# Regrouping the token blocks of a hybrid decoder step from 3+3+3 to 3+4+2, with a second buffer pool for the last group

## The chip, the core and the metric

One core of a Trainium2 chip runs the whole program. The time is that of one execution on the device, in microseconds; a run's number is the median of its executions. The engines named below are TensorE (PE; its weight loads are listed apart as PEld), VectorE (DVE), ScalarE (ACT), GpSimd (POOL) and SyncE (SP), which here only issues DMAs. Each engine works through its own list of instructions in order and waits on semaphores; which instruction stands where in a list is fixed when the program is built.

## The reference

One layer is run for a prompt of 1024 tokens and for a sample group of 8 x 8 tokens, with the same weights, everything in float32. Cut to what matters:

```python
n = rmsnorm(x, g_mix)
z = n @ w_in                      # 1024 x 7192: GLA, FoX, memory queries, three gates
h = x + (sum over b of sigmoid(gate_b) * (branch_b(n) @ w_b)) @ w_out
q = rmsnorm(h, g_ffn) @ w_pq      # 8 heads, two halves of 128
s1, s2 = q_half @ k1.T, q_half @ k2.T
v1, i1 = top_k(s1, 16); v2, i2 = top_k(s2, 16)
sc, pos = top_k(v1[:, None] + v2[None, :], 16)     # 16 of 16384 experts per head
g = softmax(sc)
a = gelu(x . u_tab[idx])          # 128 experts per token
h = h + sum (g * a) * v_tab[idx]
y = rmsnorm(h, g_final)
```

Two ways lead through the expert part. A block of 128 tokens can fetch, for each of its 128 expert slots, one row of `u` and one of `v` per token by an indirect DMA and work on them with VectorE (it is gathered). Or it can run all 16384 experts as dense matmuls against a weight matrix that is zero except at the chosen experts (it goes through the tables).

## The kernel before

The tokens are nine blocks: prompt blocks 0 to 7 of 128 tokens, and block S with the 64 sample tokens. `GROUPS` runs them in three groups through `base` (line 633), which reads every weight matrix once per group: input projection, the three branches, the gates, `w_out`, the second norm, `w_pq` and the key products. Each weight piece of 128x512 is split into a rounded part `wh` (ScalarE, line 265) and a rest `wl` (VectorE, line 267); three matmuls then stand for one. Two kinds of projection use it: `proj` puts 256 weight columns through one block at a time, `proj_T` (`jobs_T`, lines 273 to 277) puts all tokens of the group, NT of them, through 128 weight columns, so the width of its matmuls is NT. With the key products the scores of each head go to VectorE, where `top16` (lines 932 to 936) takes the 16 best of 128 twice per head and block; the blocks in `LATER` store their scores and do this inside `choose` instead.

`choose` picks the 16 pairs per head and their softmax weights. For a gathered block `peer_gather` follows (lines 1052 to 1094): 128 times an indirect DMA on POOL's queue (line 1065) brings u rows, which VectorE multiplies and sums (line 1067), and 128 times v rows (line 1076), which VectorE accumulates (line 1082). Four row buffers are shared by the two, a fifth is added in the last phase, and one block's gather follows the other. For a block in `DENSE`, `expert_weights` (line 1096) builds the weight matrix: one-hot rows on VectorE and ScalarE, a matmul into the PSUM tile `cw`, an eviction to the tile `stg` (line 1143), and after 16 tokens a DMA of `stg` to DRAM (`c_scr`). The sample block's weights are built in the last phase.

The last phase, `peer_dense` (lines 1148 to 1256), runs the 128 expert tiles for the 448 tokens of `DENSE`: per tile 8 transposes of `u`, 24 matmuls with `u` and 24 with `v`, all 448 wide. It starts when `early.close()` has given back the pools of the first part. Beside it the remaining gathered blocks are gathered.

What sets the order is a scheduler at build time with one priority per instruction. `base` of all groups counts up from zero and goes first; `choose` and `expert_weights` of the earlier groups start at half a million (`urgent`) and fill in; the gathers lie at a million and more and take what is left. So before, blocks 0, 1 and 2 are gathered beside the second and third `base`, and 6 and 7 beside the dense phase. Tiles of the first part come from the pool `bp`, whose tags hold a fixed number of buffers (`BUFS`, `CB`); `wr` holds raw weight pieces and the sample's cache pages, `P` wide scratch.

Of the kernel before, what the change touches and what calls it, by code (L numbers as in the profile page):

```python
# [18 lines left out]
F32 = mybir.dt.float32  # L19
# [19 lines left out]

ROWS, ROWS2 = 4, 5  # L40
SAMPLE = 8
GROUPS = [[0, 1, 2], [3, 4, 5], [SAMPLE, 6, 7]]

DENSE = [3, 4, 5, SAMPLE]

LATER = [6, 7]

HERE = [SAMPLE]
DG, DW = 8, 9
WR = 4  # L50
CB = {"hot": 4, "stg": 1, "eg": 1}


@with_exitstack
def tile_hybrid(ctx: ExitStack, tc: tile.TileContext, x_prompt, x_sample, cache_fox_k, cache_fox_v,
# [10 lines left out]
    dp = ctx.enter_context(tc.tile_pool(name="dp", bufs=1, space=bass.MemoryType.DRAM))  # L66
    gp = ctx.enter_context(tc.tile_pool(name="gp", bufs=1))
    early = ctx.enter_context(ExitStack())
    ec = early.enter_context(tc.tile_pool(name="ec", bufs=1))
    pp = early.enter_context(tc.tile_pool(name="pp", bufs=8, space=bass.MemoryType.PSUM))  # L70
    bp = early.enter_context(tc.tile_pool(name="bp", bufs=1))

    BUFS = {"aT": 2, "wr": WR, "wh": 4, "wl": 2, "z": 4, "zq": 1, "zt": 4, "tq": 2, "tp": 3, "oT": 3, "kv": 2, "pg": 2,
            "la": 2, "ge": 3, "lh": 4, "kE": 2, "gq": 1, "att": 2, "X": 2, "XL": 2, "P": 4, "PT": 3, "sm": 12,
            "sm2": 1, "sm5": 1}
    PSB = {"pj": 2, "g": 2, "f": 2, "po": 1, "cw": 1}
    cnt = [0]

    def T(tag, shape, dt=F32):
        cnt[0] += 1  # L80
        return bp.tile(shape, dt, tag=tag, name=f"{tag}_{cnt[0]}", bufs=BUFS[tag])

    def const(shape, dt=F32, pool=ec):
        cnt[0] += 1
# [538 lines left out]
    s_scr = {b: dp.tile([128, 2048], F32, name=f"s_scr{b}") for b in LATER}  # L623
    e_scr = {b: dp.tile([128, 128], I32, name=f"e_scr{b}") for b in DENSE}
    g_scr = {b: dp.tile([128, 128], F32, name=f"g_scr{b}") for b in DENSE}
    c_scr = dp.tile([sum(64 if b == SAMPLE else 128 for b in DENSE) // 16, 128, 2048], F32, name="c_scr")
    q_scr = dp.tile([128, 4, 64], F32, name="q_scr")
    x2_scr = [dp.tile([128, 1024], F32, name=f"x2_scr{b}") for b in range(9)]

    gate_scr = [dp.tile([12, 128, 2, 384], F32, name=f"gate_scr{i}") for i in range(len(GROUPS))]  # L630
    o_scr = [dp.tile([128, 3, 4, 128], F32, name=f"o_scr{b}") for b in range(9)]

    def xsrc(b):
# [4 lines left out]
    def base(grp):  # L638
# [64 lines left out]

        gscr = gate_scr[GROUPS.index(grp)]
        gates = gate_jobs()
# [5 lines left out]
        for half in range(2):  # L711
# [56 lines left out]
            def fin_k(b, p):  # L768
# [11 lines left out]
                evac(kT[:, :, b * 128:(b + 1) * 128], pt[:, :256].rearrange("p (j t) -> p j t", t=128))  # L780
                if b < 7 and grp is not GROUPS[-1]:
                    SP.dma_start(kT_scr[half * 256:(half + 1) * 256, b * 128:(b + 1) * 128].rearrange(
# [161 lines left out]
    def choose(b):  # L944

        if b not in DENSE:
            eidx[b] = gp.tile([128, 128], I32, tag="ei", name=f"ei{b}", bufs=2)
            gate_w[b] = gp.tile([128, 8, 16], F32, tag="gw", name=f"gw{b}", bufs=2)
        for hf in range(2):
# [52 lines left out]
            c = slice(hf * 64, (hf + 1) * 64)  # L1002
            if b in DENSE:
                ei, gw = w[:, 528:592].bitcast(I32), region(656, 16)
# [91 lines left out]
    def expert_weights(b, H=None, psum=None):  # L1096

        w = 64 if b == SAMPLE else 128
        o = sum(64 if x == SAMPLE else 128 for x in DENSE[:DENSE.index(b)]) // 16

        def H_base(tag, shape, dt=F32):
            cnt[0] += 1
            return bp.tile(shape, dt, tag=tag, name=f"{tag}_{cnt[0]}", bufs=CB[tag])

        H = H or H_base
        psum = psum or (lambda: PS("cw"))


        q, e, f = H("hot", [128, 2, 128]), H("hot", [128, 2, 128]), H("hot", [128, 2, 128])
        qi = q[:, 0].bitcast(I32)  # L1110
        SP.dma_start(qi, e_scr[b])
        SP.dma_start(q[:, 1], g_scr[b])
        V.tensor_scalar(e[:, 0].bitcast(I32), qi, 7, None, op0=OP.logical_shift_right)
        V.tensor_scalar(e[:, 1].bitcast(I32), qi, 127, None, op0=OP.bitwise_and)
        V.tensor_copy(f, e.bitcast(I32))
        p = psum()
        for i, src in enumerate((f[:, 0], f[:, 1], q[:, 1])):
            PE.transpose(p[:, i * 128:(i + 1) * 128], src, ident)

        eg = H("eg", [128, 4, 128])  # L1120
        for i in range(4):
            j = min(i, 2)
            A.activation(eg[:, i, :w], p[:, j * 128:j * 128 + w], AF.Copy, scale=-1.0 if i == 3 else 1.0)
        for sb in range(w // 16):
            stg = H("stg" if H is H_base else "c", [128, 128, 16])
            for q2 in range(8):
                ts = [sb * 16 + q2 * 2 + i for i in range(2)]
                o2, o1 = H("hot", [128, 2, 128]), H("hot", [128, 2, 128])
                for i, t in enumerate(ts):
                    if q2 % 2:  # L1130
                        V.tensor_scalar(o2[:, i], iof, eg[:, 1, t:t + 1], eg[:, 2, t:t + 1], op0=OP.is_equal,
                                        op1=OP.mult)
                    else:

                        A.activation(o2[:, i], iof, AF.Square, scale=-1.0, bias=eg[:, 1, t:t + 1])
                        A.activation(o2[:, i], o2[:, i], AF.Relu, scale=eg[:, 3, t:t + 1], bias=eg[:, 2, t:t + 1])
                V.tensor_tensor(
                    o1, iof[:, None, :].to_broadcast([128, 2, 128]),
                    eg[:, 0, ts[0]:ts[0] + 2, None].to_broadcast([128, 2, 128]), op=OP.is_equal)
                p = psum()  # L1140
                for i, t in enumerate(ts):
                    PE.matmul(p[:, i * 128:(i + 1) * 128], o2[:, i], o1[:, i], start=True, stop=True)
                A.activation(stg[:, :, q2 * 2:q2 * 2 + 2].rearrange("p n t -> p t n"),
                             p[:, :256].rearrange("p (t n) -> p t n", t=2), AF.Copy)
            SP.dma_start(c_scr[o + sb], stg.rearrange("p n t -> p (n t)"))

    def peer_dense(ctx2, dn):
# [31 lines left out]
        for b in DENSE:  # L1179
            if b in GROUPS[-1]:  # L1180
                expert_weights(b, DT, lambda: DP("c"))
# [16 lines left out]
        for g in range(128 // DG):  # L1198
            if g * DG % 8 == 0:
                c8 = DT("c", [128, NS, 128])  # L1200
                ready = NS - sum(w for b, w in zip(DENSE, widths) if b in GROUPS[-1]) // 16
                for x in (slice(0, ready), slice(ready, NS)) if g == 0 else (slice(0, NS),):
# [261 lines left out]

    for grp in GROUPS:
        pj3[0] = grp is GROUPS[0]
        base(grp)
        mine = [b for b in grp if b not in DENSE]
        first = [b for b in grp if b in DENSE]
        if grp is not GROUPS[-1]:  # L1470
            first = mine[:1] + first
        else:
            first += mine[:1]
        for b in first:
            if b in DENSE and grp is GROUPS[-1]:
                choose(b)
            else:
                at(None, choose, b)
            if b in DENSE and grp is not GROUPS[-1]:
                at(None, expert_weights, b)  # L1480
        if mine and grp is not GROUPS[-1]:
            gather(mine)
# [38 lines left out]
```

## Time and profile before

| what | value |
|---|---|
| three runs | 4328.08, 4340.33, 4341.13 us (median 4340.33) |
| the profiled execution | 4325.89 us |
| its span, first to last instruction | 4324.1 us |
| mean granted TensorE clock | 0.909 of full |
| PE busy | 3719.4 us (86%) |
| DVE busy | 3338.8 us (77%) |
| ACT busy | 1821.1 us (42%) |
| POOL busy | 1691.6 us (39%) |
| HBM read and written | 1086.8 and 77.1 MB |

The shares are means over stages with different limits. The page's line of 40 slices shows it at a glance: PE stands at 8 and 9 in the first slices and at 9 from the 28th on, and between 6 and 9 in the middle, where DVE and the DMA engines stand mostly at 7 to 9. So the middle has to be read on its own, and for each engine by what it waited for.

### The profile page before, as it was taken

What the parts mean: (1) busy time and instruction counts of PE and PEld (TensorE: products, weight loads), DVE (VectorE), ACT (ScalarE), POOL (GpSimd) and SP (SyncE); (2) the same over time, 40 slices, a digit from 0 to 9 for tenths busy, and PEclk for the clock granted to TensorE, in tenths of its full rate; (3) what the DMA queues carried; (4) which work ended last, traced back from release to release, by engine and by line L of the source; (5) the groups of instructions that cost most, each with busy time, mean ns of one, the idle gap of its engine ahead of it and who ended that gap; (6) DMA issues with size and microseconds to landing.
All of it is one profiled execution on the core that took longest, in us unless ns stands there. A gap on an engine that the chain in (4) does not pass through costs nothing. (4 is left out here: it accounts for less than half of the span.)

```text
span 4324.1 us, 62414 instructions
## 1 busy us (share of the span) xinstructions
PE 3719.4 (86%) x21306; PEld 3260.5 (75%) x21306; DVE 3338.8 (77%) x7924; ACT 1821.1 (42%) x3710; POOL 1691.6 (39%) x1466
## 2 busy tenths in 40 slices
PE   4999898779777876887888976867999999999997
PEld 4989797768656774776665656756998899889997
DVE  3444479988779898988865458988998888788883
ACT  2565544345444324665664434353332233223322
POOL 0000003554454445446454544414444445454440
PEclk9999998889778976896889998988999999999999
DMA  3334457989889977888888899968989999899992
GB/s 112 109 101 142 138 166 246 307 259 324 282 307 322 307 250 250 285 271 285 286 275 297 282 342 341 321 214 311 310 303 330 338 335 332 315 330 340 342 310 83
DMA packets 665781, 1168.08 MB, mean 270 GB/s; under 512 B 63309, under 2 KB 453093, under 8 KB 661878
## 3 DMA queue, kind: packets, MB, share of 16 engines
q0 software_dynamic: 193616, 704.99, 46.7%
q1 hardware_dynamic: 471846, 459.09, 32.7%
q8 instruction: 169, 2.77, 0.2%
q14 instruction: 150, 1.23, 0.1%
HBM read 1086.82 MB, written 77.11 MB: 269 GB/s over the span
## 5 line engine op out<-in xcount | busy, mean ns | idle before, releaser
L1065 POOL DMA_INDIRECT u<-in_peer_u_dram,ei x640 | 787.2, 1230 | 863.4 <-DVE a L1067 391.2
L1076 POOL DMA_INDIRECT v<-in_peer_v_dram,ei x640 | 764.8, 1195 | 871.5 <-DVE acc L1082 411.7
L1082 DVE SCALAR_TENSOR_TENSOR acc<-v,a,acc 128x1024 f32<-128x1024 f32 x635 | 812.7, 1280 | 68.5 <-DMA v<-in_peer_v_dram,ei 65.5
L1067 DVE CUSTOM_DVE_ANT_0 u<-u,x 128x1024 f32<-128x1024 f32 x640 | 774.4, 1221 | 76.8 <-DMA u<-in_peer_u_dram,ei 76.2
L265 ACT ACTIVATE wh<-wr 128x512 fp32r<-128x512 f32 x568 | 354.3, 630 | 551.8 <-PE pj L274 175.5
L267 DVE TENSOR_TENSOR wl<-wr,wh 128x512 fp32r<-128x512 f32 x568 | 388.7, 688 | 156.7 <-PE pj L277 54.1
L1235 PE MATMUL py<-dwh,dvh 128*128 128x448 f32 x1024 | 375.4, 370 | 35.1 <-ACT dwh L1222 31.0
L1212 PE MATMUL pa<-xh,duh 128*128 128x448 f32 x1024 | 384.5, 375 | 3.9 <-ACT duh L1193 3.9
L273 PE MATMUL pj<-aT,wh 128*128 128x384 f32 (+1 forms) x1104 | 373.6, 344 | 12.1 <-ACT tq L99 7.3
L1213 PE MATMUL pa<-xl,duh 128*128 128x448 f32 x1024 | 380.2, 371 | 0.0
L1236 PE MATMUL py<-dwl,dvh 128*128 128x448 f32 x1024 | 376.0, 368 | 1.5 <-DVE dwl L1223 1.5
L1237 PE MATMUL py<-dwh,dvl 128*128 128x448 f32 x1024 | 374.1, 368 | 2.0 <-DVE dvl L1231 2.0
L274 PE MATMUL pj<-aT,wh 128*128 128x384 f32 (+1 forms) x1104 | 367.9, 337 | 1.5 <-DVE aT L317 1.5
L1230 ACT ACTIVATE dvh<-dvr 128x1024 fp32r<-128x1024 f32 x128 | 134.0, 1058 | 394.1 <-PE py L1236 191.8
L281 PE MATMUL pj<-wh,aT 128*128 128x256 f32 x944 | 263.4, 303 | 36.0 <-DVE z L888 8.8
L282 PE MATMUL pj<-wh,aT 128*128 128x256 f32 x944 | 261.4, 299 | 6.6 <-DVE aT L872 5.3
L277 PE MATMUL pj<-aT,wl 128*128 128x384 f32 (+1 forms) x1104 | 261.6, 341 | 5.8 <-DVE wl L267 5.8
L1215 PE MATMUL pa<-xh,dul 128*128 128x448 f32 x1024 | 239.4, 369 | 0.0
L1235 PEld LDWEIGHTS py<-dwh,dvh 128*128 128x128 f32 x1024 | 192.5, 189 | 52.2 <-ACT dwh L1222 31.2
L273 PEld LDWEIGHTS pj<-aT,wh 128*128 128x128 f32 x1104 | 217.2, 197 | 19.2 <-ACT tq L99 11.4
L281 PEld LDWEIGHTS pj<-wh,aT 128*128 128x128 f32 x944 | 193.4, 206 | 43.0 <-DVE z L739 8.2
L274 PEld LDWEIGHTS pj<-aT,wh 128*128 128x128 f32 x1104 | 217.6, 197 | 2.8 <-DVE aT L317 2.4
(489 smaller groups left out, 8328.5 us busy)
## 6 DMA issues: line engine op xcount, KB each, us to landing
wr<-in_w_in_dram SPq DMA_DIRECT2D x168, 512.0 KB, 5.1
dvr<-in_peer_v_dram SPq DMA_DIRECT2D x128, 512.0 KB, 7.1
dur<-in_peer_u_dram SPq DMA_DIRECT2D x128, 512.0 KB, 6.3
dc<-c_scr SPq DMA_DIRECT2D x15, 1792.0 KB, 16.7
wr<-in_w_pq_dram SPq DMA_DIRECT2D x48, 512.0 KB, 5.7
c_scr<-stg SPq DMA_DIRECT2D x24, 1024.0 KB, 6.3
wr<-in_w_out_dram SPq DMA_DIRECT2D x24, 512.0 KB, 6.4
u<-in_peer_u_dram,ei POOLq DMA_INDIRECT x640, 6.3
```

The costliest lines, as they stand in the source:

```text
L267: V.tensor_tensor(wl, raw[:, q2:q2 + 2], wh.bitcast(F32), op=OP.subtract)
L273: PE.matmul(ps, wh[:, i, c], hi[:, k], start=k == 0, stop=False)
L274: PE.matmul(ps, wh[:, i, c], lo[:, k], start=False, stop=False)
L281: PE.matmul(ps, hi[:, k, :], wh[:, i], start=k == 0 and first, stop=False)
L1065: G.indirect_dma_start(out=r, out_offset=None, in_=UR, in_offset=bass.IndirectOffsetOnAxis(ap=ei[:, s:s + 1], axis=0))
L1067: V.tensor_tensor_reduce(r, r, x2, 1.0, 0.0, OP.mult, OP.add, a[:, s:s + 1])
L1076: G.indirect_dma_start(out=r, out_offset=None, in_=VR, in_offset=bass.IndirectOffsetOnAxis(ap=ei[:, s:s + 1], axis=0))
L1082: V.scalar_tensor_tensor(acc, r, a[:, s:s + 1], acc, op0=OP.mult, op1=OP.add)
L1212: PE.matmul(pa[:, :NT], uh[:, k], xh[:, k], start=k == 0, stop=False)
L1213: PE.matmul(pa[:, :NT], uh[:, k], xl[:, k], start=False, stop=False)
L1235: PE.matmul(py[:, :NT], vh[:, j], wh, start=j == 0, stop=False)
L1236: PE.matmul(py[:, :NT], vh[:, j], wl, start=False, stop=False)
```

## The change

Block 6 moves from the third group into the second: 0, 1, 2 / 3, 4, 5, 6 / S, 7. NT goes from 384, 384, 320 to 384, 512, 192. Block 3 is now gathered and block 6 goes through the tables, so 0, 1, 2, 3 and 7 are gathered and 4, 5, 6, S are dense; the numbers of gathers and of dense columns stay the same, but block 3 is ready for its gather after the second group, and only block 7 has to wait for the last phase. After the `base` of the second group the pool `bp` is closed and a new one, `bq`, opened in its place; `wr` then has 6 buffers (4 before), `P` 6 (4 before), and `stg` 2 (1 before, in all of `expert_weights`). The count of instructions on the compute engines is the same but for a few table loads on ACT.

```diff
@@ -39,16 +39,16 @@
 
 ROWS, ROWS2 = 4, 5
 SAMPLE = 8
-GROUPS = [[0, 1, 2], [3, 4, 5], [SAMPLE, 6, 7]]
-
-DENSE = [3, 4, 5, SAMPLE]
-
-LATER = [6, 7]
+GROUPS = [[0, 1, 2], [3, 4, 5, 6], [SAMPLE, 7]]
+
+DENSE = [4, 5, 6, SAMPLE]
+
+LATER = [7]
 
 HERE = [SAMPLE]
 DG, DW = 8, 9
 WR = 4
-CB = {"hot": 4, "stg": 1, "eg": 1}
+CB = {"hot": 4, "stg": 2, "eg": 1}
 
 
 @with_exitstack
@@ -68,7 +68,8 @@
     early = ctx.enter_context(ExitStack())
     ec = early.enter_context(tc.tile_pool(name="ec", bufs=1))
     pp = early.enter_context(tc.tile_pool(name="pp", bufs=8, space=bass.MemoryType.PSUM))
-    bp = early.enter_context(tc.tile_pool(name="bp", bufs=1))
+    layer = early.enter_context(ExitStack())
+    bps = [layer.enter_context(tc.tile_pool(name="bp", bufs=1))]
 
     BUFS = {"aT": 2, "wr": WR, "wh": 4, "wl": 2, "z": 4, "zq": 1, "zt": 4, "tq": 2, "tp": 3, "oT": 3, "kv": 2, "pg": 2,
             "la": 2, "ge": 3, "lh": 4, "kE": 2, "gq": 1, "att": 2, "X": 2, "XL": 2, "P": 4, "PT": 3, "sm": 12,
@@ -78,7 +79,7 @@
 
     def T(tag, shape, dt=F32):
         cnt[0] += 1
-        return bp.tile(shape, dt, tag=tag, name=f"{tag}_{cnt[0]}", bufs=BUFS[tag])
+        return bps[0].tile(shape, dt, tag=tag, name=f"{tag}_{cnt[0]}", bufs=BUFS[tag])
 
     def const(shape, dt=F32, pool=ec):
         cnt[0] += 1
@@ -627,7 +628,7 @@
     q_scr = dp.tile([128, 4, 64], F32, name="q_scr")
     x2_scr = [dp.tile([128, 1024], F32, name=f"x2_scr{b}") for b in range(9)]
 
-    gate_scr = [dp.tile([12, 128, 2, 384], F32, name=f"gate_scr{i}") for i in range(len(GROUPS))]
+    gate_scr = [dp.tile([12, 128, 2, 512], F32, name=f"gate_scr{i}") for i in range(len(GROUPS))]
     o_scr = [dp.tile([128, 3, 4, 128], F32, name=f"o_scr{b}") for b in range(9)]
 
     def xsrc(b):
@@ -1100,7 +1101,7 @@
 
         def H_base(tag, shape, dt=F32):
             cnt[0] += 1
-            return bp.tile(shape, dt, tag=tag, name=f"{tag}_{cnt[0]}", bufs=CB[tag])
+            return bps[0].tile(shape, dt, tag=tag, name=f"{tag}_{cnt[0]}", bufs=CB[tag])
 
         H = H or H_base
         psum = psum or (lambda: PS("cw"))
@@ -1465,6 +1466,11 @@
     for grp in GROUPS:
         pj3[0] = grp is GROUPS[0]
         base(grp)
+        if grp is GROUPS[-2]:
+
+            layer.close()
+            bps[0] = layer.enter_context(tc.tile_pool(name="bq", bufs=1))
+            BUFS.update(wr=6, P=6)
         mine = [b for b in grp if b not in DENSE]
         first = [b for b in grp if b in DENSE]
         if grp is not GROUPS[-1]:
```

In the lists of instructions this shows at three places. The rows below give line, operation, output and inputs; the line numbers of the changed kernel are one higher up to its main loop. The first place is TensorE's list where the second group ends and the third begins. Before, the key products of the second group (line 915, `tq` into `f`) are mixed with the transposes of the third group's tokens (line 314, `wr` into `g`) and its first projection (line 273, 320 wide):

```order
L277 MATMUL pj_15993<-aT_15042,wl_16049 128x384 x2
L277 MATMUL pj_15994<-aT_15042,wl_16049 128x384 x2
L314 MATMUL g_18641<-c_76,wr_18632 128x128 x4
L314 MATMUL g_18648<-c_76,wr_18632 128x128 x4
L915 MATMUL f_15852<-c_257,tq_15815 128x128 x2
L314 MATMUL g_18664<-c_76,wr_18655 128x128 x4
L273 MATMUL pj_18828<-aT_18606,wh_18832 128x320
L273 MATMUL pj_18829<-aT_18606,wh_18832 128x320
L314 MATMUL g_18671<-c_76,wr_18655 128x128 x4
L915 MATMUL f_15942<-c_257,tq_15939 128x128 x2
```

In the change, the last key products of all four blocks come first, and the third group's transposes and first projection (192 wide) stand behind them:

```order
L916 MATMUL f_17326<-c_257,tq_17323 128x128 x2
L916 MATMUL f_17343<-c_257,tq_17323 128x128 x2
L916 MATMUL f_17360<-c_257,tq_17323 128x128 x2
L916 MATMUL f_17377<-c_257,tq_17323 128x128 x2
L315 MATMUL g_20853<-c_76,wr_20843 128x128 x4
L315 MATMUL g_20860<-c_76,wr_20843 128x128 x4
L315 MATMUL g_20876<-c_76,wr_20867 128x128 x4
L315 MATMUL g_20883<-c_76,wr_20867 128x128 x4
L274 MATMUL pj_20991<-aT_20841,wh_20995 128x192
```

What was interleaved is now one after the other.

The second place is SyncE's queue at the same point, with the waits. Before, the third group's tokens are loaded (line 324) while top-16 lists (`tp`) of the second group are still being stored to `t_scr`:

```order
L925 DMA t_scr_287<-tp_15451 128x64 [waits DVE_49]
L925 DMA t_scr_288<-tp_15468 128x64 [waits DMAHW7_49,DVE_49]
L324 DMA wr_18608<-in_x_sample_dram 64x1024 [waits DMAHW0_49,Pool_49]
L324 DMA wr_18632<-in_x_prompt_dram 128x1024 [waits DMAHW2_49,DMAHW1_49,DVE_49]
L324 DMA wr_18655<-in_x_prompt_dram 128x1024 [waits DMAHW0_49,DVE_49,PE_49]
L262 DMA wr_18830<-in_w_in_dram 128x4x256 [waits DMAHW3_49,DVE_49,Activation_49]
L925 DMA t_scr_289<-tp_15485 128x64 [waits DMAHW4_49,DVE_49]
```

In the change the first load of the third group (line 339, the gains) stands behind the last store and waits for all eight DMA counters, ScalarE and GpSimd; the tokens (line 325) and weights follow it:

```order
L926 DMA t_scr_289<-tp_17365 128x64 [waits DMAHW1_49,DVE_49]
L926 DMA t_scr_290<-tp_17382 128x64 [waits DMAHW2_49,DVE_49]
L339 DMA kv_20839<-in_g_mix_dram 128x1024 [waits DMAHW3_49,DMAHW4_49,DMAHW2_49,DMAHW5_49,DMAHW1_49,DMAHW6_49,DMAHW0_49,DMAHW7_49,Activation_49,Pool_49]
L325 DMA wr_20867<-in_x_prompt_dram 128x1024
L263 DMA wr_20993<-in_w_in_dram 128x4x256
L263 DMA wr_21027<-in_w_in_dram 128x4x256
L325 DMA wr_20843<-in_x_sample_dram 64x1024 [waits Pool_49]
```

The loads of the third group have moved behind the last use of the closed pool.

The third place is VectorE's list a little ahead of the dense phase. Before, the last gathered block of the first group (block 2: `acc`, then line 1041) ends beside `choose` of the sample block (`ch`), and the token splits of the dense phase (`xl`) follow:

```order
L1082 SCALAR_TENSOR_TENSOR acc_8963<-v_9643,a_8860,acc_8963 128x1024
L935 MAX last_t<-zt_26347 128x8 x2
L1008 TENSOR_SCALAR ch_0_26371<-ch_0_26371 128x64
L1010 TENSOR_SCALAR ch_0_26371<-ch_0_26371 128x64
L1041 TENSOR_TENSOR acc_8963<-acc_8963,h_9646 128x1024
L936 MAX_INDEX last_t<-last_t,zt_26347 128x8 x2
L1009 SCALAR_TENSOR_TENSOR ch_0_26371<-ch_0_26371 128x64
L1013 TENSOR_TENSOR ch_0_26371<-ch_0_26371 128x64
L1016 TENSOR_REDUCE ch_0_26371<-ch_0_26371 128x4
```

In the change block 3 is in the middle of its gather there, and its u rows (line 1068, listed as two rows each) stand between the same instructions:

```order
L937 MAX_INDEX last_t<-last_t,zt_27386 128x8 x2
L1068 ISA u_20209,a_20041<-u_20209,x_4230_20039 128x1024
L1068 ISA a_20041 128x1
L1001 MATCH_REPLACE ch_0_27404<-ch_0_27404 128x50 x8
L1068 ISA u_20215,a_20041<-u_20215,x_4230_20039 128x1024
L1068 ISA a_20041 128x1
L1068 ISA u_20212,a_20041<-u_20212,x_4230_20039 128x1024
L1068 ISA a_20041 128x1
L1002 MAX ch_0_27404<-ch_0_27404 128x8 x8
L1068 ISA u_20218,a_20041<-u_20218,x_4230_20039 128x1024
L1068 ISA a_20041 128x1
```

Gather work of a fourth block has moved ahead of the dense phase.

## Rows read from the trace of the kernel before

**Rows 1.** Windows by stage: stretch and length, busy us per engine, PE clock, DMA, GB/s.

```profile
0.00:660.00 660.00, 572.77 (x3800) 534.16 (x3801) 322.90 (x982) 330.22 (x697) 20.31 (x50) 0.96 0.42 128
660.00:1480.00 820.00, 650.10 (x3692) 565.13 (x3690) 702.15 (x1777) 350.94 (x724) 404.02 (x347) 0.83 0.88 298
1480.00:1560.00 80.00, 60.73 (x313) 55.13 (x314) 78.85 (x281) 28.35 (x58) 35.80 (x33) 0.83 0.84 269
1560.00:2500.00 940.00, 778.87 (x4639) 606.90 (x4640) 722.04 (x1968) 507.44 (x1170) 470.73 (x388) 0.85 0.82 277
2500.00:2850.00 350.00, 259.60 (x1561) 222.16 (x1560) 282.17 (x656) 130.58 (x268) 141.00 (x128) 0.87 0.94 326
2850.00:2960.00 110.00, 67.66 (x372) 59.50 (x371) 91.14 (x399) 58.86 (x137) 23.55 (x23) 0.80 0.65 223
2960.00:4200.00 1240.00, 1227.47 (x6415) 1125.08 (x6414) 1086.92 (x1808) 379.90 (x606) 591.65 (x492) 1.00 0.94 328
4200.00:4324.00 124.00, 102.17 (x527) 92.41 (x525) 52.64 (x62) 34.80 (x54) 4.55 (x10) 0.92 0.33 101
660.00:2850.00 2190.00, 1749.29 (x10201) 1449.32 (x10200) 1785.22 (x4679) 1017.31 (x2218) 1051.56 (x893) 0.85 0.86 292
```

**Rows 2.** One line at a time: durations min/median/max in ns, first and last start.

```profile
L1212 PE MATMUL pa<-xh,duh x1024: 362/368/722, 2846.1 to 4257.1; 128*128 128x448 f32 x171
L1082 DVE SCALAR_TENSOR_TENSOR acc<-v,a,acc x635: 1256/1280/1330, 762.2 to 4204.8; 128x1024 f32<-128x1024 f32 x159
```

**Rows 3.** The same view, 1400 to 1700 us: norms of third group, top-16 of second.

```profile
L329 DVE SCALAR_TENSOR_TENSOR wr<-wr,sm,kv x3: 1267/1280/1285, 1513.2 to 1522.9; 128x1024 f32<-128x1024 f32 x3
L935 DVE MAX8 tp<-zt x48: 256/284/304, 1457.1 to 1620.3; 128x8 f32<-128x128 f32 x48
```

**Rows 4.** VectorE groups by shape: busy us, mean ns, idle before and its releaser.

```profile
L1082 DVE SCALAR_TENSOR_TENSOR acc<-v,a,acc 128x1024 f32<-128x1024 f32 x635 | 812.7, 1280 | 68.5 <-DMA v<-in_peer_v_dram,ei 65.5 <-DVE dwl L1223 0.4
L1067 DVE CUSTOM_DVE_ANT_0 u<-u,x 128x1024 f32<-128x1024 f32 x640 | 774.4, 1221 | 76.8 <-DMA u<-in_peer_u_dram,ei 76.2
L1067 DVE DVE_READ_ACCUMULATOR2_ANT a<- 128x1 f32 x640 | 54.2, 85 | 0.0
L935 DVE MAX8 tp<-zt 128x8 f32<-128x128 f32 x96 | 24.2, 287 | 0.0
L1001 DVE MAX8 ch<-ch 128x8 f32<-128x50 f32 x144 | 20.9, 201 | 0.0
```

**Rows 5.** TensorE in order of time: start, duration, line, tiles, shape, count.

```profile
91.76 0.37 PE L686 MATMUL f<-P,aT 128*128 128x24 f32 x1
91.97 0.37 PE L684 MATMUL f<-P,aT 128*128 128x24 f32 x1
...
178.07 0.34 PE L274 MATMUL pj<-aT,wh 128*128 128x384 f32 x1
178.25 0.34 PE L562 MATMUL f<-c,c 128*128 128x128 f32 x2
178.42 0.39 PE L273 MATMUL cw<-aT,wh 128*128 128x384 f32 x1
```

**Rows 6.** Waits of VectorE, 660 to 2850 us: total us, times, longest.

```profile
DVE hot L1131 <- PE cw L1142: 63.6, 32, 10.6
DVE acc L1082 <- DMA v<-in_peer_v_dram,ei: 63.3, 54, 4.0
DVE u L1067 <- DMA u<-in_peer_u_dram,ei: 61.6, 69, 4.3
```

**Rows 7.** Waits of ScalarE, then of GpSimd, in the same stretch.

```profile
ACT wh L265 <- DMA wr<-in_w_in_dram: 34.8, 9, 21.7
ACT stg L1143 <- DMA c_scr<-stg: 27.8, 14, 4.3
POOL wr L1262 <- PE g L1326: 38.6, 25, 3.5
```

## The prediction

> **What bounds the kernel now.** I read the windows by stage first [rows 1]. They cut the run into a first group of about 660 us (PE 573 busy, gathers not yet begun), a mixed part from 660 to 2850 us, a handover of 110 us to 2960, and a dense phase of 1240 us with a tail of 124. The dense phase is TensorE's: 1227 of 1240 us busy at the full clock. The first matmul with u in the dense phase starts at 2846 us and the last at 4257, and the last accumulation of a gathered row at 4205 us [rows 2]. So the two gathers beside the dense phase are hidden, with some 50 us to spare, and a gather that leaves that phase frees nothing that the end waits for. What counts is when the dense phase can start, and that is decided in the mixed part. There no engine is full: PE 1749 of 2190 us (80%, at 0.85 of the clock), VectorE 1785 (82%), the DMA engines 0.86. Each engine works down a fixed list, and projections, expert weights and gathers of three blocks wait for each other. VectorE is nearest to its limit where no sample attention runs: 702 of 820 us, then 79 of 80 around the end of the second group.
>
> **The change part by part.** All durations are from the profiled execution of 4325.9 us, 14 us under the median of the three runs (4340.3).
>
> *The end of the second group.* Before, the third group's norms run at 1513 to 1523 us, while the second group's top-16 goes on until 1620 [rows 3]: 107 us in which the two overlap. In the changed lists the first load into the new pool waits for everything that used the old one, and queued behind it on SP are the third group's tokens and weights, for which ScalarE, VectorE and TensorE wait in turn. Between the last weight split of the second group and the third group's first norm, VectorE's list holds 32 accumulations of v rows, one u row, 146 top-16 instructions and 42 small ones of `choose`. By [rows 4] that is 32 x 1.280 = 41.0, 1.3, 146 x 0.287 = 41.9 and 42 x 0.201 = 8.4, 93 us in all, in which TensorE has only the last key products. Bounds: nothing, if VectorE is what limits all along, since this work has to be done somewhere; 107 us, the whole overlap. PE is busy 60.7 of 80 us at that place before [rows 1]; 0.76 of 93 to 107 us is 70 to 81. I take 75.
>
> *More gathering ahead of the dense phase.* Before, 398 u rows and 384 v rows stand in VectorE's list ahead of the first dense product with the weight matrix; in the change 448 and 426. The 50 u rows cost 50 x (1.221 + 0.085) = 65 us and the 42 v rows 42 x 1.280 = 54 us [rows 4], 119 in all. One u and 32 v rows, 42 us, lie in the gap just counted; 77 us remain. VectorE is idle for 405 of 2190 us, so the lower bound is 0, all of it in idle time. The upper one is the pace at which gathers went there: 768 in 2190 us are 2.85 us each, and 59 of them 168 us. With one share of idle of 14% in one stage and 23% in another I take half of the 77, 38 us. Every moved row also takes its DMA on POOL's queue along, with the same bounds.
>
> *Top-16 and choosing.* One more block does its top-16 with its group, and block 3 is chosen ahead of the dense phase, while block 6's top-16 and half its choosing go: by the lists 46 top-16 instructions x 0.287 = 13 and 142 small ones x 0.201 = 29, 42 us of VectorE. Most stands in the gap already counted or in idle time; 0 to 42, I take 10.
>
> *Buffers.* ScalarE waited 27.8 us for `stg` to be stored, in 14 of 24 stores [rows 7]; behind it `cw` stands still, and part of VectorE's 63.6 us of waiting for `cw` [rows 6] follows. Two buffers take this away: 0 to 64, I take 20 off. ScalarE waited 34.8 us for `w_in`, and the sample's page loads held up POOL's queue, with the gathers behind them, for 38.6 us [rows 7]. Six `wr` buffers help in the last group alone: 0 to 73 off, I take 15.
>
> *Widths.* 1536 matmuls go from 384 to 512 columns and 1536 from 320 to 192. A 384-wide one starts 173 to 180 ns after its predecessor, and two 128-wide ones take 170 together [rows 5]. The line through 85 and 173 ns gives 0.34 ns per column; the sum of columns does not change, so the cost is 0. A rival below doubts this.
>
> *The dense phase* has 92 fewer gathers beside it. PE lost 12.5 us in 1240; at most that comes back, I take 8 off.
>
> Sum: 75 + 38 + 10 - 20 - 15 - 8 = +80 us, 4406 us against the profiled execution and 4420 against the median. I say 4415.
>
> **A rule weighed against the rows.** The DMA engines were 0.94 busy at 326 GB/s from 2500 to 2850 us [rows 1], so the rows say that full engines move some 347 GB/s here, and 92 rows of 512 KB, 48 MB, would then take 140 us if they found no gap. The Trainium skill (HBM Reference, Specifications) states about 425 GB/s for a core that streams alone. By that rate the same bytes would take 113 us. The trace does not reach it anywhere in those stages; its own rate decides. Both speak against bringing gathers forward, and neither says whether they find a gap: 0.14 of 2190 us, 307 us, was free.
>
> **The rivals.**
>
> *The mixed part takes it all in (faster).* The extra 119 + 42 us of VectorE fit into its 405 idle us, and TensorE makes good the gap, because the third group has a block less and VectorE is free of top-16 when it starts. Then only gains remain: 27.8 + 34.8 + 12.5 = 75 us, 4251 us; half of them gives 4288. It decides if the first dense matmul comes before 2840 us. For it: from 1560 to 2500 us VectorE is idle for 218 us. Against it: the order of the lists is fixed, and the gap stands in TensorE's own list.
>
> *Gains and gap cancel:* within 13 us of before.
>
> *The gathers set the pace.* If the 59 gathers outside the gap cost their 2.85 us each, and the gap 107, the sum is 107 + 168 + 10 - 43 = +242, 4568 us; with the gap at 75, 4536. For it: VectorE's 125 us of waiting for u and v rows [rows 6], and DMA at 0.94 in the last stretch. Against it: those waits are 6% of the part.
>
> *Narrow matmuls are slow.* 24-wide products start 210 ns apart, two and a half times as far as 128-wide ones [rows 5]. If 192 fell on the slow side, at 210 to 300 ns instead of 107, 1536 of them would add 158 to 296 us: 4564 to 4702. The 128-wide row speaks against it.
>
> **How the numbers follow.** The forecast case, a slowdown of some 25 to 170 us (4350 to 4500), has 0.61; taking it all in 0.18; cancelling 0.07; the gathers' pace 0.11; narrow matmuls 0.03. A measurement of this kernel tells about 0.3%, 13 us, from no change. So faster 0.18, same 0.07, slower 0.75. The range from 4290 to 4520 us leaves out about half of the first rival, most of the gathers' pace and the narrow matmuls, under 2 in 10; the likeliest case's own range is 4350 to 4500.
>
> **What would show it.** Right: in the changed profile TensorE nearly idle for 70 us or more between the last key product of the second group and the first transpose of the third, its clock down behind it; the first dense matmul at 2900 to 3000 us; the dense phase as long as before and still PE's at 99%; no wait of ScalarE for `stg`; the last gathered row well before the last expert. Wrong: a gap under 40 us, or a mixed part no longer than 2190 us in spite of it (the idle time took the gathers in); a dense phase shorter by over 15 us (the gathers did cost TensorE something there); 192-wide products over 150 ns apart.

## The result: 179 us slower, and the profile after

The changed kernel takes 4519.97 us (median of 4 runs, 4514.95 to 4526.86) against 4340.73 us for the kernel before (median of 4): a ratio of 1.0433, 95% interval 1.0408 to 1.0458. The forecast was 4415 us. The direction holds. The size does not: +179 us where the sum gave +80.

First TensorE by stage in the changed kernel, as [rows 1] have it of before: stretch and length, busy us of PE, PEld, DVE, ACT and POOL, PE's clock, DMA share, GB/s. The stretches are the gap at the end of the second group, its last 48 us, the mixed part, the handover and the dense phase.

```profile
1800.00:1930.00 130.00, 34.08 (x122) 26.13 (x120) 109.13 (x441) 15.19 (x32) 45.39 (x47) 0.59 0.74 217
1880.00:1928.00 48.00, 0.00 (x0) 0.00 (x0) 30.71 (x91) 5.25 (x10) 15.74 (x18) 0.50 0.82 240
660.00:3027.00 2367.00, 1809.32 (x10204) 1439.67 (x10204) 1895.58 (x5059) 1027.63 (x2232) 1104.30 (x960) 0.81 0.85 284
3027.00:3144.00 117.00, 72.63 (x342) 62.66 (x341) 109.50 (x381) 53.58 (x125) 49.87 (x46) 0.69 0.87 305
3144.00:4459.00 1315.00, 1297.67 (x6763) 1190.08 (x6764) 1002.72 (x1497) 398.28 (x640) 496.05 (x406) 0.99 0.82 281
```

The first dense matmul and the last accumulated row, the lines that answer to [rows 2]:

```profile
L1213 PE MATMUL pa<-xh,duh x1024: 362/368/722, 3027.3 to 4458.9; 128*128 128x448 f32 x171
L1083 DVE SCALAR_TENSOR_TENSOR acc<-v,a,acc x635: 1254/1277/1346, 767.4 to 4167.3; 128x1024 f32<-128x1024 f32 x159
```

The first dense matmul comes at 3027 us instead of 2846, and the last at 4459 instead of 4257. So 181 of the 202 us are lost ahead of the dense phase. The handover, from the first dense matmul to the first weighted product, grows from 99 us (2846 to 2945) to 117, and the dense phase behind it is no shorter (1312 before, 1315 now), though its last gathered row now comes 290 us ahead of the last matmul with u instead of 50.

The gap, in TensorE's order of time: start, duration, line, tiles, shape, count, and the idle time before with its releaser. L278 is a projection of the second group, L916 its key products, L315 the first transposes of the third group.

```profile
1830.99 1.09 PE L278 MATMUL pj<-aT,wl 128*128 128x512 f32 x4
1831.92 0.61 PE L916 MATMUL f<-c,tq 128*128 128x128 f32 x4
...
1877.87 1.22 PE L916 MATMUL f<-c,tq 128*128 128x128 f32 x4 [3.76 <-ACT zt L100]
1928.11 1.12 PE L315 MATMUL g<-c,wr 128*128 128x128 f32 x4 [49.02 <-DMA kv<-in_state_gla_dram]
```

From the last projection to the first transpose TensorE has 96 us with a few key products in them. VectorE has no such hole in the first 77 of them, where it is busy for 72; from its list there:

```profile
1858.98 1.26 DVE L1083 SCALAR_TENSOR_TENSOR acc<-v,a,acc 128x1024 f32<-128x1024 f32 x1
1860.16 0.08 DVE L937 MATCH_VALUE_LOAD tp<-tp,zt 128x8 f32 x1
1860.23 0.28 DVE L937 FIND_INDEX8 tp<-tp,zt 128x8 uint32<-128x128 f32 x1
...
1861.67 1.27 DVE L1083 SCALAR_TENSOR_TENSOR acc<-v,a,acc 128x1024 f32<-128x1024 f32 x1
```

Gathered rows stand between the top-16 instructions on which the closing of the pool waits: 29 of them, 35.5 us of the 72. The last 19 us are another matter. They run from the first load that the closing held back (SyncE's queue) to the first transpose. VectorE is busy for only 5 of them and waits for the rest, while the DMA engines are full (share 1.01 of the window):

```profile
1908.68 0.33 SPq L339 DMA_DIRECT2D kv<-in_g_mix_dram  x1
1926.77 1.28 DVE L330 SCALAR_TENSOR_TENSOR wr<-wr,sm,kv 128x1024 f32<-128x1024 f32 x1 [4.67 <-POOL sm L307]
```

So the gap is a backlog of 77 us and a restart of 19, in which tokens are loaded and normed.

### The profile page after: what moved, and what is told of

It is laid out like the page before. It is cut to its first block, busy times and chain, and to the rows that moved or that the text cites. A ratio compares the mean times of both kernels' runs of the same rounds, so it can differ in the third digit from the quotient of the medians.

```text
span 4525.1 us, 62526 instructions
## 1 busy us (share of the span) xinstructions
PE 3797.0 (84%) x21306; PEld 3266.1 (72%) x21306; DVE 3350.2 (74%) x7924; ACT 1824.0 (40%) x3712; POOL 1672.7 (37%) x1466
## 5 line engine op out<-in xcount | busy, mean ns | idle before, releaser
L1066 POOL DMA_INDIRECT u<-in_peer_u_dram,ei x640 | 777.7, 1215 | 802.3 <-DVE a L1068 384.1
L274 PE MATMUL pj<-aT,wh 128*128 128x512 f32 (+2 forms) x1104 | 378.7, 355 | 14.5 <-ACT tq L100 6.1
L275 PE MATMUL pj<-aT,wh 128*128 128x512 f32 (+2 forms) x1104 | 372.9, 349 | 1.1 <-DVE aT L318 1.1
L278 PE MATMUL pj<-aT,wl 128*128 128x512 f32 (+2 forms) x1104 | 275.9, 354 | 22.0 <-DVE wl L268 21.6
L274 PEld LDWEIGHTS pj<-aT,wh 128*128 128x128 f32 x1104 | 222.5, 202 | 38.4 <-ACT tq L100 9.9
L275 PEld LDWEIGHTS pj<-aT,wh 128*128 128x128 f32 x1104 | 222.9, 202 | 19.4 <-DVE aT L318 2.0
L278 PEld LDWEIGHTS pj<-aT,wl 128*128 128x128 f32 x1104 | 191.5, 201 | 46.7 <-DVE wl L268 27.6
```

Source lines behind the costliest of these rows:

```text
L274: PE.matmul(ps, wh[:, i, c], hi[:, k], start=k == 0, stop=False)
L275: PE.matmul(ps, wh[:, i, c], lo[:, k], start=False, stop=False)
L278: PE.matmul(ps, wl[:, i, c], hi[:, k], start=False, stop=k == kt - 1)
L1066: G.indirect_dma_start(out=r, out_offset=None, in_=UR, in_offset=bass.IndirectOffsetOnAxis(ap=ei[:, s:s + 1], axis=0))
```

## The experiments

The theory after the result: the closing costs some 60 us, block 3's rows ahead of the dense phase most of the rest. Rivals: the gathers set the pace (2.8 us a row), or the grouping, the widths or the choice of block 3 cost what I had put at little or nothing. Differences below are between medians and their own runs of the kernel before.

**Block 3 chosen and gathered behind block 7.** 787 rows then stand ahead of the first weighted product of the dense phase; before has 782, the change 874.

```
-        if grp is not GROUPS[-1]:            # for `first`
+        if grp is GROUPS[0]:
...
-        else:
+        elif grp is GROUPS[-1]:
...
-        if mine and grp is not GROUPS[-1]:   # for `gather`
+        if mine and grp is GROUPS[0]:
...
-            gather(mine)                     # the last one
+            gather(mine + [3])
```

> The changed kernel with one thing moved: block 3 is chosen and gathered in the last phase, behind block 7, so that ahead of the dense phase's first weighted product VectorE's list holds 787 gathered rows (782 in the kernel before, 874 in the changed one). Groups, pool switch and buffers stay as changed. If the gathers set the pace of the mixed part (2.8 us each there in both profiles), 87 fewer take off about 240 us at most and some 180 as the whole change cost: 4330 to 4370 us. If the switch of pools and the regrouping are what costs, and gathers are mostly hidden, 4460 to 4510 us. My prediction's own terms (75 for the gap, 38 for the gathers) would give some 4470.

Measured: 4411.89 us, ratio 1.0198 [1.0162, 1.0233], 82 above before. Block 3's early choice and gathering are worth 97 us together; none of the three expectations held.

**The closing alone**, in the kernel before, with its groups, widths and buffers.

```
+        if grp is GROUPS[-2]:
+            layer.close()
+            bps[0] = layer.enter_context(tc.tile_pool(name="bq", bufs=1))
```

> The kernel before with one part of the change alone: the pool is closed after the second group and a new one with the same buffers opened; groups, gathers and buffers as before (787 rows ahead of the dense phase against 782). If the empty stretch of TensorE at the switch costs its length, 75 to 107 us: 4415 to 4445 us. If gathers set the pace and go on during the gap, 0 to 30 us: 4340 to 4370 us.

Measured: 4387.68 us, 1.0137 [1.0096, 1.0178], +58, between the two expectations. Its gap:

```profile
1547.39 0.94 PE L278 MATMUL pj<-aT,wl 128*128 128x384 f32 x4
1553.95 1.23 PE L916 MATMUL f<-c,tq 128*128 128x128 f32 x4 [5.61 <-ACT zt L100]
...
1594.10 1.23 PE L916 MATMUL f<-c,tq 128*128 128x128 f32 x4 [2.67 <-ACT zt L100]
1647.58 1.97 PE L315 MATMUL g<-c,wr 128*128 128x128 f32 x8 [52.26 <-DVE wr L330]
```

99 us without a projection cost 58. The last norm of the third group comes 128 us later than before (1650.6 against 1522.9), the first dense matmul 70 (2915.7 against 2846.0). So the third group gives 58 us back, 1265 against 1323 between the two, probably because no top-16 of the second group runs beside it; no run shows that cause.

**64 rows less** in the kernel before (the last two heads of block 2).

```
+HEADS = {2: 6}
...
-        for hd in range(8):
+        nh = HEADS.get(b, 8)
+        for hd in range(nh):
```

> The kernel before, with the last two of the eight heads of block 2 left out of its gather (32 rows of u and 32 of v; that block's output lacks them), so 64 fewer gathered rows in the mixed part and nothing else changed. If gathers set the pace there, 64 times 2.8 us = 180 us less: 4160 us. If they fill idle time, 0 to 40 us less: 4300 to 4340 us; half of VectorE's time for them, as in the prediction, would be 41 us less.

Measured: 4291.78 us, 0.9915 [0.9887, 0.9943], 38 us less (25 to 49 by the interval), 0.59 us a row. The pace theory, some 2.8 us a row, falls; half of VectorE's time for a row fits.

**Block 3 chosen early, gathered last.** The first run with the choice put back to its place in the changed kernel.

```
-        if mine and grp is not GROUPS[-1]:
+        if grp is GROUPS[0]:
...
-            gather(mine)
+        gather(mine)
+        at(prio[0] + M, peer_gather, 3)
```

> The changed kernel with the choice of block 3's experts left where it is, behind the second group, but its gathering moved behind block 7's, at the very end. 787 rows are then taken in ahead of the first dense product instead of 874, as in the run that deferred both (4412 us). Theory 'rows': the 87 rows ahead of the dense phase cost the 108 us, the choice nothing: 4400 to 4430 us. Theory 'choice': the 12 us of VectorE per half of the choice, with its waits, sits in the path of the third group: 4480 to 4520 us. Half and half gives 4440 to 4475.

Measured: 4444.05 us, 1.0265 [1.0234, 1.0295], +111, as 'half and half' had it. The choice costs 28 us (111 - 82), the early gathering 68 (179 - 111).

**The old buffers** in the changed kernel: `stg` 1 in place of 2, and no `BUFS.update(wr=6, P=6)`.

> The changed kernel with the buffer counts of before (wr 4, P 4, stg 1) and nothing else undone. My prediction put the buffers at -35 us (stg -20, wr and P -15): by that the time is 4545 to 4565 us. Rival: the buffers hide nothing, since VectorE's queue and TensorE set the pace: 4510 to 4530 us.

Measured: 4532.76 us, 1.0461 [1.0426, 1.0496], +199. That lies between the two expectations. The buffers are worth some 12 to 20 us, by ratios or by medians, with overlapping intervals. Not all of it need be the buffers: the order of the lists moves with them, and in this run 893 rows start ahead of the first weighted product, 19 more than in the changed kernel, which at 0.6 us a row are 11 us. ScalarE's waits from 660 to 3050 us, here and then in the changed kernel:

```profile
ACT wh L266 <- DMA wr<-in_x_sample_dram: 34.3, 1, 34.3
ACT stg L1144 <- DMA c_scr<-stg: 25.6, 8, 5.6
ACT wh L266 <- DMA wr<-in_w_in_dram: 18.7, 12, 3.1
```

```profile
ACT wh L266 <- DMA wr<-in_w_in_dram: 50.7, 8, 33.0
```

The wait for `stg` goes, as forecast. The one for `w_in` does not. Its longest piece, 33 us in the changed kernel, ends at 1920 us: it is the gap at the closing, and in this run the same wait stands in the first row (34.3), since there another load came last. Outside the gap ScalarE waits 17.7 us for `w_in` with six `wr` buffers and 18.7 with four, so the two more save next to nothing there. The piece of 21.7 us in the kernel before [rows 7] is gone in both.

**Nearly without rows**, three kernels: the changed one, the one before, and the one before with the closing, each with `HEADS` of 1 for its gathered blocks up to block 3.

> The changed kernel with only the first of eight heads gathered in blocks 0 to 3 (32 rows a block, 224 a block left out). What is left is the cost of the grouping, the closing of the pool and the widths nearly without gathering beside them. Theory 'the closing and the regrouping cost about 80 us whatever is gathered': 70 to 95 us above the kernel before with the same heads left out. Theory 'the closing is only a loss because the gathers in the gap cannot use TensorE, and the regrouping is free': 0 to 50 us above it. If a row costs 1.24 us in the changed kernel over its whole range, this runs at 3590 to 3650 us; at 0.6 us a row, 4050 to 4100 us.

> The kernel before with only the first of eight heads gathered in blocks 0 to 2 (224 rows a block left out, 686 of them ahead of the first dense product). At 0.59 us a row, the slope of the run with 64 rows less, 3930 us; if that slope belongs to the last rows only and most of the mixed part is bounded by TensorE and its chains, 4050 to 4200 us.

> The kernel before with the closed pool (same buffers) and one of eight heads gathered in blocks 0 to 2. Without the closing that kernel ran at 3915 us, the changed one with the same heads left out at 3986. Theory 'the gap costs the same whatever is gathered': 3965 to 3985 us, so that regrouping and widths are worth nothing with few rows. Theory 'gathers fill part of the gap, and without them it costs its full length': 4000 to 4030 us, and regrouping is a gain.

Measured: 3985.55 us for the changed one (0.9228 [0.9184, 0.9272]), 3915.01 for the one before (0.9036 [0.9007, 0.9064]), 3946.31 with the closing (0.9110 [0.9089, 0.9132]). The 672 rows left out of the kernel before (3 x 224, 667 of them ahead of the first weighted product; the 686 of the expectation is too many) make it 418 us faster, 0.62 us a row, so the slope of the last 64 holds for nearly all. The changed kernel is 71 us above the one before, as the theory of the same cost whatever is gathered had it (70 to 95), but with all rows that difference is 179. The closing costs 31 us with few rows, under both expectations, and 58 with all; the interval of that difference is some 23 us wide on either side. The grouping and the rest cost 39 with few, against 121 (179 - 58) with all. So the theory that rows fill the gap falls: where they stand in it, they lengthen it. The gap of the closing with few rows:

```profile
1410.25 0.96 PE L279 MATMUL pj<-aT,wl 128*128 128x384 f32 x4
1411.44 1.16 PE L917 MATMUL f<-c,tq 128*128 128x128 f32 x8 [0.23 <-ACT tq L101]
1413.80 0.71 PE L917 MATMUL f<-c,tq 128*128 128x128 f32 x4 [1.20 <-ACT zt L101]
1441.01 1.97 PE L316 MATMUL g<-c,wr 128*128 128x128 f32 x8 [26.50 <-DVE wr L331]
```

30 us instead of 99: here the key products do not lag behind the projections. The loads that end the backlog and begin the restart, with few rows and then in the closing alone with all:

```profile
1427.76 0.33 SPq L340 DMA_DIRECT2D kv<-in_g_mix_dram  x1
```

```profile
1630.72 0.33 SPq L339 DMA_DIRECT2D kv<-in_g_mix_dram  x1
```

The backlog, from the last projection to this load, is 17 us instead of 82, with no row in it; the restart is 13 instead of 17. But the changed kernel with few rows has a gap of 74 us:

```profile
1608.51 1.21 PE L279 MATMUL pj<-aT,wl 128*128 128x512 f32 x4
...
1683.89 1.97 PE L316 MATMUL g<-c,wr 128*128 128x128 f32 x8 [46.16 <-DVE wr L331]
```

Its first load is issued at 1665.72 us, so 56 us are backlog. VectorE has 12 u rows and some 12 v rows there, some 29 us, and about as much top-16. So the length of the gap goes by what stands in VectorE's list when the group ends, top-16 and rows alike, and not by how many rows the kernel gathers. How much of the 39 us this longer gap makes, no run separates.

**What of a row costs.** First the changed kernel with 96 rows of block 3 (`HEADS = {3: 3}`), then the same with little VectorE work on them, then with few fetches, where VectorE multiplies `x2` by itself in place of the missing row.

```
# little work
+                n = 32 if b == 3 else 1024
+                V.tensor_tensor_reduce(r[:, :n], r[:, :n], x2[:, :n], ...)
...                                      # the same for v
# few fetches (u and v)
+                if b != 3 or k == 0:
+                    r = big("u")
+                    G.indirect_dma_start(out=r, ...)
+                V.tensor_tensor_reduce(r, x2 if b == 3 else r, x2, ...)
...                                      # the same condition for v
```

> The changed kernel with three of block 3's eight heads gathered (160 rows left out, nearly all of them rows of the dense phase; 862 rows stand ahead of the first dense product instead of 874). It is the baseline of the two runs beside it. If rows in the dense phase are free, 4495 to 4520 us; if they cost there what they cost in the mixed part, 4380 to 4430.

> The run with 96 rows of block 3, but VectorE works on 32 of 1024 columns of each of them: the rows are fetched as before, about 110 us of VectorE's work goes. Theory 'VectorE': a row costs what VectorE spends on it, so 70 to 110 us below the baseline, at 4400 to 4440 us. Theory 'fetching' (GpSimd's issues, queues and traffic set the price): within 20 us of the baseline, about 4500.

> The run with 96 rows of block 3, but only one row in sixteen is fetched; VectorE works in full on what is there. Theory 'VectorE': within 20 us of the baseline, about 4500 us. Theory 'fetching': 70 to 110 us below it.

Measured: 4493.69 us (1.0362 [1.0341, 1.0382]), just under the range for free rows; with little work 4461.87 (1.0300 [1.0272, 1.0329]); with few fetches 4511.68 (1.0412 [1.0392, 1.0431]). Taking VectorE's work away gains 32 us of the 92 that it had been busy (3166.3 to 3074.1): less than one theory's 70 and more than the other's 20. Taking the fetches away gains nothing, it is 18 us slower, which I can't explain. So the price of these rows is in the main VectorE's, a third to a half of its busy time, and no run shows one of the fetching. The first of the three also shows that the other 160 rows, 148 of them beside the dense phase, are not free: without them the kernel is 19 us faster (160 against 179), by the ratios 31. The 12 that stand ahead would make 8 of it at 0.65 us a row.

Where these 19 to 31 us lie is seen in the windows of two kernels beside those of the changed one above. The run with block 3 chosen early and gathered last, handover and dense phase:

```profile
2987.00:3086.00 99.00, 61.93 (x340) 54.67 (x339) 85.74 (x387) 51.57 (x124) 24.84 (x23) 0.76 0.73 260
3086.00:4376.00 1290.00, 1287.74 (x6749) 1186.52 (x6750) 1090.08 (x1517) 399.81 (x640) 597.60 (x493) 1.00 0.92 320
```

The run with 96 rows of block 3, the same two:

```profile
3042.00:3141.00 99.00, 67.52 (x342) 58.90 (x340) 92.79 (x323) 52.77 (x124) 33.04 (x31) 0.79 0.87 303
3141.00:4437.00 1296.00, 1289.94 (x6755) 1187.07 (x6756) 835.03 (x1311) 400.62 (x636) 314.03 (x260) 1.00 0.68 225
```

With some 490 gathers beside it (the column of POOL) the dense phase is shorter (1290 us) than the changed kernel's with some 400 (1315), while before, with as many as the first, it took 1312. So not their number counts, and what makes these 20 us stays open. The handover is 18 us longer in the changed kernel. It has 46 gathers there, against 23 and 31, and TensorE waits longer for the weights that VectorE prepares, by its waits in the handover of the changed kernel and of the run gathered last (9.9 us in the run with 96 rows):

```profile
PE pc L1143 <- DVE dhot L1138: 21.7, 17, 5.3
```

```profile
PE pc L1143 <- DVE dhot L1138: 6.7, 5, 2.3
```

The granted clock is lower there too, 0.69 against 0.76 and 0.79, and the same 340 matmuls keep TensorE busy for 73 us instead of 62 and 68. That the rows in the handover are the cause is argued and not shown: the run with the old buffers has 44 there and a handover as long (120 us), but that wait is only 9.3 us in it.

## Why the prediction was right in direction and wrong in size

In short: the gap and the price of a row came out nearly as forecast; the terms that stood at nothing or at a gain (widths, buffers, choice, dense phase) did not. The runs form a chain from the kernel before to the changed one. Busy and idle (span less busy) are TensorE's in the profiled executions.

| kernel | median to before | TensorE busy, idle | step |
|---|---|---|---|
| before | 0 | 3719, 605 | |
| closing alone | +58 | 3727, 660 | closing 58 |
| block 3 all behind 7 | +82 | 3755, 657 | groups, widths, buffers 24 |
| block 3 chosen early | +111 | 3773, 671 | choice 28 |
| 96 rows of block 3 early | +160 | 3789, 715 | 75 rows ahead 49 |
| changed | +179 | 3797, 728 | other rows of block 3 19 |

An interval of a ratio is about 0.2 to 0.4% wide on either side, 9 to 18 us, so a step is known to some 14 to 23 us, and the smaller steps are only just clear of noise. The steps depend on each other, as the runs with few rows show. The step of 49 also leaves 160 rows of block 3 out, so it is the price of 75 rows only as far as those cost nothing beside the dense phase.

- *The end of the second group* (75): 58. The mechanism was in the main the one described: 96 us between the last projection and the first transpose, in which VectorE works off top-16, choosing and rows. But it is busy there for 72 us and not for the 93 that I had added up, and the 19 us of restart, which bring the gap to its length all the same, were not in the sum: that part is luck. The weighting by 0.76 gave a little too much.
- *More gathering* (38 for 59 rows outside the gap): 49 for 75. Half of VectorE's time was about right, 0.65 us a row here and 0.59 to 0.62 in the kernel before. The rival in which the gathers set the pace, 168 us for 59 rows, is refuted by three runs.
- *Top-16 and choosing* (10): the choice of block 3 alone costs 28. I had taken a quarter of 42 us and should have kept near the upper bound. I had put most of it into the gap or into idle time. But between the profiles without and with this choice, the third group's last norm comes 13 us later (1922.6 and 1935.6) and the first dense matmul 43 (2944.1 and 2987.0), so more of the delay arises in the third group, behind the gap; what waits for it there was not tested.
- *Buffers* (-35): -12 to -20, part of which may be the moved rows. The 20 for `stg` may be right. For the 15 of `wr` there is no sign: six buffers left the wait for `w_in` outside the gap as it was (17.7 against 18.7 us), and the 21.7 us of it that I had counted on went without them.
- *Widths* (0): with the buffers, this is where the sum failed most. Together I had them at -35; the step from the closing alone to block 3 all behind 7, which holds groups, widths and buffers, measured +24 (known to some 23 us), 59 of the 99 us between sum and result. With the buffers' 12 to 20 taken out, grouping and widths cost some 36 to 44 us. 28 us of that is TensorE's busy time; that all of it reaches the total is argued. Its three lines of projections, in the run with block 3 all behind 7 and then in the closing alone (busy us, mean ns):

```profile
L274 PE MATMUL pj<-aT,wh 128*128 128x512 f32 (+2 forms) x1104 | 380.1, 356 | 9.0 <-ACT tq L100 4.1 <-ACT kv L100 2.9 <-ACT aT L317 0.7
L275 PE MATMUL pj<-aT,wh 128*128 128x512 f32 (+2 forms) x1104 | 373.3, 349 | 0.0
L278 PE MATMUL pj<-aT,wl 128*128 128x512 f32 (+2 forms) x1104 | 273.9, 352 | 18.8 <-DVE wl L268 18.7
```

```profile
L274 PE MATMUL pj<-aT,wh 128*128 128x384 f32 (+1 forms) x1104 | 374.6, 344 | 19.2 <-ACT tq L100 9.9 <-ACT wh L266 4.7 <-ACT kv L100 3.2
L275 PE MATMUL pj<-aT,wh 128*128 128x384 f32 (+1 forms) x1104 | 368.1, 337 | 0.0
L278 PE MATMUL pj<-aT,wl 128*128 128x384 f32 (+1 forms) x1104 | 262.5, 341 | 5.5 <-DVE wl L268 5.3
```

1027 against 1005 us, 22 more for the same columns in all. The starts show why. At the full clock, products of 320 columns in the kernel before are 0.147 us apart:

```profile
1760.12 0.31 PE L274 MATMUL pj<-aT,wh 128*128 128x320 f32 x1
...
1760.71 0.31 PE L274 MATMUL pj<-aT,wh 128*128 128x320 f32 x1
```

(four steps), those of 384 in the closing alone 0.173:

```profile
1536.82 0.33 PE L275 MATMUL pj<-aT,wh 128*128 128x384 f32 x1
...
1537.86 0.33 PE L275 MATMUL pj<-aT,wh 128*128 128x384 f32 x1
```

(six steps), and in the changed kernel those of 512 are 0.228 (five steps) and those of 192 are 0.110 apart:

```profile
1787.65 0.39 PE L274 MATMUL pj<-aT,wh 128*128 128x512 f32 x1
...
1788.79 0.39 PE L275 MATMUL pj<-aT,wh 128*128 128x512 f32 x1
...
1936.80 0.27 PE L274 MATMUL pj<-aT,wh 128*128 128x192 f32 x1
1936.91 0.28 PE L275 MATMUL pj<-aT,wh 128*128 128x192 f32 x1
```

512 and 192 take 0.338 together, 384 and 320 take 0.320: 18 ns for each of 1536 pairs are 28 us. My line of 0.34 ns per column was right at 192 (0.107) and 11 ns too low at 512 (0.217); from 320 columns up a column costs 0.42 ns. The rival of slow narrow matmuls, +158 to +296 us, is refuted all the same. It rested on a row that I misread: the 24-wide products of [rows 5], 0.21 us apart, ran at a granted clock of 0.50 (91 to 93 us). At 1.00 (687.5 to 688.5 us) the same products start 0.11 apart, like the 192-wide ones:

```profile
687.58 0.26 PE L685 MATMUL f<-P,aT 128*128 128x24 f32 x1
687.69 0.26 PE L686 MATMUL f<-P,aT 128*128 128x24 f32 x1
```

The rest of this step, some 8 to 16 us, was not measured alone.

- *The dense phase* (-8): +19 to +31 by the run without those 160 rows; by the profiles of before and after +3 in the dense phase and +18 in the handover. I counted rows that leave it, and not that block 3's rows, now in front of block 7's, fall into the handover. No step of the sum spoke of the handover.

The errors are -17, +11, +18, +15 to 23, +36 to 44 and +27 to 39: five of six on the same side. That by the medians they come to 98 of the 99 us between sum and result says nothing more, since the chain's steps add up to the whole by the way it is built. No single step carries all of the error. The steps that I set to nothing, or to a gain, without a bound above nothing were the costly ones.

Of the signs that I had named, these held: the clock down behind the gap; no wait for `stg`; the last row well before the last expert; a dense phase as long as before; 192-wide products under 150 ns apart at the full clock. TensorE is nearly idle for over 70 us if one counts from the last projection (96); from the last key product, as I had worded it, it is 49 us, between my sign of right and that of wrong. The first dense matmul came at 3027 us and not at 2900 to 3000.

No experiment points to a version that beats the kernel before: the closing costs 58 us and the buffers that it makes room for are worth 12 to 20. The changed groups without the closing, and the kernel before with the larger buffers, have no run here.

## What to carry to other kernels

Where one engine lags behind at a stage's end, a barrier leaves the others idle for its backlog, and for the restart of what it held back (82 and 17 us here, of which 58 were lost): look at what else stands in that engine's list there, since such work doesn't fill the gap but lengthens it. A wait that a barrier makes can stand under the name of any load behind it, so look at when it ended before putting it down to buffers. A step that the trace prices at "hidden" needs its bounds on both sides like any other, and many small ones of the same sign make a large error. Ask of every transfer that is moved into which hand-over between stages it falls: here the handover with more rows in it was the longer one.

## What the hardware showed that I had not expected

The 192-wide products that follow the gap of 49 us in the changed kernel are slower than those shown above, which stand 2.4 us behind these:

```profile
1934.37 0.41 PE L274 MATMUL pj<-aT,wh 128*128 128x192 f32 x1
1934.59 0.41 PE L275 MATMUL pj<-aT,wh 128*128 128x192 f32 x1
```

They start 0.21 us apart and then 0.11. The granted clock in the last 48 us of the gap is 0.50, the lower of its two levels (1.2 GHz), and it stays there from 1928 to 1936 us, so the gap also slows what follows it, for some 8 us. That the clock would be down behind the gap was among my signs; how soon it is back was not. At half the rate over 8 us this loses some 4 us by my estimate, a small part of what the closing costs.
